# Transposing the FFN's hidden activations in 32x32 blocks on VectorE

## The chip, the cores and the metric

The kernel runs on one core of a Trainium2 chip. The metric is the device time of one execution in microseconds (us), taken as the median of several runs. The engines are TensorE (PE in the profile, PEld for its weight loads), VectorE (DVE), ScalarE (ACT), GpSimd (POOL) and SyncE (SP, which here only issues transfers).

## What is computed

One hybrid decoder layer on 256 tokens of width 2048, in float32: a half-step SwiGLU, a mixer (three attention groups side by side), and a second half-step SwiGLU. The change concerns the two SwiGLU blocks, which are these lines of the reference (D_MODEL = 2048, D_FF = 5632):

```
def swiglu(x, w_gate, w_up, w_down):
    return (jax.nn.silu(x @ w_gate) * (x @ w_up)) @ w_down
...
    x = x + 0.5 * swiglu(rms_norm(x, ffn1_norm[l]), ffn1_gate[l], ffn1_up[l], ffn1_down[l])
...
    x = x + 0.5 * swiglu(rms_norm(x, ffn2_norm[l]), ffn2_gate[l], ffn2_up[l], ffn2_down[l])
```

The hidden activations h = silu(gate) * up come out with tokens on the partitions, and the product with w_down needs them with the hidden index on the partitions. So h, 256 x 5632, is transposed once in each block.

## The kernel before, in words

**Precision by splitting.** Every weight and every activation that enters a large matmul is kept as two fp32r tiles: `hi`, a cast of the value, and `lo`, the value minus `hi`. A product is three matmuls: hi·hi, hi·lo, lo·hi (`mm_rows`, L272, L273, L274). A weight batch is 256 rows by 512 columns (`KB` = 2 tiles of 128 rows): one transfer from SP's queue into a tile `raw` (L218; four buffers), a cast on ACT into `hi` (L220; three buffers), a subtraction on DVE into `lo` (L221; three buffers), then 12 matmuls of 128x512, two token tiles by two row tiles by three. The second of the 12 is the first to read `lo`.

**Names.** `ag`, `au`, `ad` are gate, up and down weights of the first block, `bg`, `bu`, `bd` of the second, with the number of the batch's first row tile behind the name: `lo_ag_6` is the fourth batch of a gate chunk. `ga` and `ua` are the PSUM accumulators of gate and up.

**The loop.** `ffn` runs 11 chunks of 512 hidden columns. For each: gate, 8 weight batches; Silu on ACT into an SBUF tile `g` (L369, two halves of 128x512); up, 8 batches; and on DVE the product of up with `g` (L373, two halves), which leaves h for this chunk in `g`, with 128 tokens on the partitions. Then the down projection runs four chunks of 512 output columns, 22 batches each, reading `hT`, the transposed and split h.

**The transpose before.** `transpose_h` puts 8 TensorE transposes of 128x128 (L348) into one PSUM tile `th`, then calls `split` twice: ACT casts 128x512 out of PSUM into hT's hi half (L225), DVE subtracts into its lo half (L226).

**What sets the order.** `Lanes.tick()` is called after each weight batch and advances the queued side jobs by one `yield`. A job given to `lanes.put` waits for one of two lanes, each with a PSUM tile; one given to `lanes.run` needs no lane. The program's order is then a scheduler's: it may move instructions on an engine unless they are wrapped in `tc.keep_in_program_order`. Each engine runs its own list strictly in order. The lists are those shown in the section on the change.

Of the kernel before, what the change touches and what calls it, by code (L numbers as in the profile page):

```python
# [8 lines left out]
F32 = mybir.dt.float32  # L9
# [7 lines left out]
P = 128  # L17
D = 2048
NK = D // P
SEQ = 256  # L20
NT = SEQ // P
# [59 lines left out]
def hybrid_layer(ctx, tc, x, mem, ffn1_norm, ffn1_gate, ffn1_up, ffn1_down, mix_norm, mem_norm,  # L81
# [3 lines left out]
    nc = tc.nc  # L85

    x, mem, out = x[0], mem[0], out[0]
# [13 lines left out]
    def psum(tag, name):  # L101

        return ps.tile([P, 2, 512], F32, tag=tag, bufs=2 if tag == "acc" else 1, name=name)

    lanes = Lanes()
# [20 lines left out]
    ident = cpool.tile([P, P], F32, name="ident")  # L126
# [97 lines left out]
    def split(dst_hi, dst_lo, src):  # L224
        nc.scalar.copy(dst_hi, src)  # L225
        nc.vector.tensor_tensor(out=dst_lo, in0=src, in1=dst_hi.bitcast(F32), op=ALU.subtract)  # L226

    def transpose_chunk(xT, src, k0, nk, g0, name, pause=1, hi_dve=False, tag2=None):
# [24 lines left out]
            yield 1  # L253
        return stages

    def square_sums(ss, src, c):
        for t in range(NT):
            junk = small.tile([P, 512], F32, tag="junk", bufs=2, name="junk")
            tc.keep_in_program_order(
                nc.scalar.activation(junk, src[:, t, :], AF.Square, accum_out=ss[:, t, c:c + 1]))  # L260
# [15 lines left out]
    def project(acc, aT, w, c0, width, kts, nk_all, done, name, before=None):  # L276

        for k0, n in kts:
            k = k0
            while k < k0 + n:  # L280
                b = min(KB, k0 + n - k)
                if before:
                    before(k)
                wh, wl = load_w(w, k, b, c0, width, f"{name}_{k}")
                for j in range(b):
                    mm_rows(acc, aT, k + j, wh[:, j, :], wl[:, j, :], done == 0, done == nk_all - 1)
                    done += 1
                k += b
                lanes.tick()
        return done  # L290

    def project_end(acc, aT, w, c0, k0, n, name, landed):


        tiles = []
        for k in range(k0, k0 + n, KB):
            wh, wl = load_w(w, k, KB, c0, 512, f"{name}_{k}")
            tiles += [(wh[:, j, :], wl[:, j, :]) for j in range(KB)]
        for t in range(NT):
            for j, (wh, wl) in enumerate(tiles):  # L300
                hi, lo = (aT[:, k0 + j, i, t * P:(t + 1) * P] for i in range(2))
                nc.tensor.matmul(acc[:, t, :], hi, wh, start=False, stop=False)
                nc.tensor.matmul(acc[:, t, :], hi, wl, start=False, stop=False)
                nc.tensor.matmul(acc[:, t, :], lo, wh, start=False, stop=j == n - 1)
            for c, width in ((0, 256), (256, 256)) if t else ((0, 512),):
                landed(t, c, width)
        lanes.tick()

    def project_first(acc, aT, w, before, ready, name):


        batches = [(k, 1) for k in range(4)] + [(k, KB) for k in range(4, NK, KB)]

        def load(i):
            k, b = batches[i]
            before(k)
            return load_w(w, k, b, 0, 512, f"{name}_{k}", None if k else first_w)

        nxt = load(0)
        for i, (k, b) in enumerate(batches):  # L320
            (wh, wl), nxt = nxt, load(i + 1) if i + 1 < len(batches) else None
            ready(k)
            if k == 0:
                for a, v in ((0, wh), (1, wh), (0, wl)):
                    for t in range(NT):
                        nc.tensor.matmul(acc[:, t, :], aT[:, 0, a, t * P:(t + 1) * P], v[:, 0, :],
                                         start=a == 0 and v is wh, stop=False)
            else:
                for j in range(b):
                    mm_rows(acc, aT, k + j, wh[:, j, :], wl[:, j, :], False, k + j == NK - 1)  # L330
            lanes.tick()


    def ffn(xT, before, ready, stats, wg, wu, wd, after, last, name):


        with tc.tile_pool(name=f"h_{name}", bufs=1, reuse_waits="tile") as hpool, \
                tc.tile_pool(name=f"ht_{name}", bufs=2, reuse_waits="tile") as htmp:
            hT = hpool.tile([P, NF, 2, SEQ], F32R, name=f"hT_{name}")

            def transpose_h(j, h):

                def stages(tag):
                    tp = psum(tag, f"th_{name}{j}")
                    tv = tp.rearrange("p a b -> p (a b)").rearrange("p (k s) -> p k s", k=4)
                    for k in range(4):
                        for t in range(NT):
                            nc.tensor.transpose(tv[:, k, t * P:(t + 1) * P], h[:, t, k * P:(k + 1) * P],  # L348
                                                ident)
                    yield 1  # L350
                    for b in range(2):
                        f = slice(4 * j + 2 * b, 4 * j + 2 * b + 2)
                        split(hT[:, f, 0, :], hT[:, f, 1, :], tv[:, 2 * b:2 * b + 2, :])
                    yield 1
                return stages

            rstd = None
            for j in range(DFF // 512):
                acc = psum("acc", f"g{name}{j}")
                if j == 0 and ready:  # L360
                    project_first(acc, xT, wg, before, ready, f"{name}g{j}")
                else:
                    project(acc, xT, wg, j * 512, 512, [(0, NK)], NK, 0, f"{name}g{j}",
                            None if j else before)
                if j == 0:
                    rstd = stats()
                g = htmp.tile([P, NT, 512], F32, tag="g", bufs=3, name=f"gs{name}{j}")
                for t in range(NT):
                    nc.scalar.activation(g[:, t, :], acc[:, t, :], AF.Silu, scale=rstd[:, t:t + 1])  # L369
                acc = psum("acc", f"u{name}{j}")  # L370
                project(acc, xT, wu, j * 512, 512, [(0, NK)], NK, 0, f"{name}u{j}")
                for t in range(NT):
                    nc.vector.scalar_tensor_tensor(out=g[:, t, :], in0=acc[:, t, :],  # L373
                                                   scalar=rstd[:, t:t + 1], in1=g[:, t, :],
                                                   op0=ALU.mult, op1=ALU.mult)
                lanes.put(f"hT{name}{j}", transpose_h(j, g))

            def before_d(k):
                if k >= NF - 4:
                    lanes.finish(f"hT{name}{DFF // 512 - 1}")  # L380

            for c in range(4):
                acc = psum("acc", f"d{name}{c}")

                def landed(t, c0, width):
                    xc = x_sb[:, t, c * 512 + c0:c * 512 + c0 + width]
                    nc.vector.scalar_tensor_tensor(out=xc, in0=acc[:, t, c0:c0 + width], scalar=0.5, in1=xc,
                                                   op0=ALU.mult, op1=ALU.add)
                    after(c, t, c0, width)

                ending = 2 if last and c == 3 else 0
                project(acc, hT, wd, c * 512, 512, [(0, NF - ending)], NF, 0, f"{name}d{c}",
                        None if c else before_d)
                if ending:
                    project_end(acc, hT, wd, c * 512, NF - ending, ending, f"{name}d{c}", landed)
                else:
                    for t in range(NT):
                        landed(t, 0, 512)
# [34 lines left out]
    def sum_stages(ss, src, c, wait=None):  # L433
        yield 2 + c if wait is None else wait
        square_sums(ss, src(c), c)
# [17 lines left out]
    def mem_stages_T(c):  # L453
        def stages(tag):
            raw = mem_raw(c)
            yield 3
            yield from transpose_chunk(lambda: memTs[0], lambda: raw, 4 * c, 4, G_MEM, f"mem{c}")(tag)
            square_sums(ssm, raw, c)
        return stages
# [11 lines left out]
    def stats0():  # L471
        lanes.finish(*(f"ss0_{c}" for c in range(4)))
        return row_rstd(ss0, "x0")

    ffn(x0T, before0, ready0, stats0, gate1, up1, down1, after1, False, "a")
    memT = memTs[0]
    lanes.finish("memT3")


    with tc.tile_pool(name="mix", bufs=1, reuse_waits="tile") as mx, \  # L480
# [51 lines left out]
        sv = slots[:, 30:32, :]  # L532
# [216 lines left out]
        for half, (a, b) in (("a", (0, 3)), ("b", (3, 6))):  # L749
            for g, (c0, dst) in enumerate(((FOX_Q, fqT), (FOX_K, fkT))):  # L750
                name = f"f{'qk'[g]}{half}"
# [45 lines left out]
    def stats2():  # L797
        lanes.finish("ss2_3")
        return row_rstd(ss2, "x2")

    ffn(x2T, lambda k: lanes.finish("bT3") if k == 12 else None, None, stats2, gate2, up2, down2, store, True, "b")


# [29 lines left out]
```

## Time and profile before

| | us |
|---|---|
| median of 3 runs | 1833.43 (1833.03 to 1834.21) |
| the profiled execution, as timed | 1832.96 |
| its span, first to last instruction | 1831.3 |
| TensorE busy | 1821.4 (99%) |
| VectorE busy | 941.2 (51%) |
| ScalarE busy | 845.6 (46%) |

The profiled execution's own time lies 1.7 us above its span and 0.5 us below the median of the runs. Matmuls are pipelined, so the busy time of a matmul group counts overlaps of its own only; the distance from start to start is what one costs. An engine's idle time in front of an instruction is shown with what ended it.

### The profile page before, as it was taken

What the parts mean: (1) busy time and instruction counts of PE and PEld (TensorE: products, weight loads), DVE (VectorE), ACT (ScalarE), POOL (GpSimd) and SP (SyncE); (2) the same over time, 40 slices, a digit from 0 to 9 for tenths busy, and PEclk for the clock granted to TensorE, in tenths of its full rate; (3) what the DMA queues carried; (4) which work ended last, traced back from release to release, by engine and by line L of the source; (5) the groups of instructions that cost most, each with busy time, mean ns of one, the idle gap of its engine ahead of it and who ended that gap; (6) DMA issues with size and microseconds to landing.
All of it is one profiled execution on the core that took longest, in us unless ns stands there. A gap on an engine that the chain in (4) does not pass through costs nothing.

```text
span 1831.3 us, 21918 instructions
## 1 busy us (share of the span) xinstructions
PE 1821.4 (99%) x8434; PEld 1534.4 (84%) x8434; DVE 941.2 (51%) x1131; ACT 845.6 (46%) x1149; POOL 11.0 (1%) x31
## 2 busy tenths in 40 slices
PE   8999999999999999999999999999999999999998
PEld 7888888888888888888999888888888888888887
DVE  5545454545545454645666455455544444544443
ACT  6444444444435444557666454444444444433332
POOL 2000000000000000000000000000000000000000
PEclk9999999999999999999999999999999999999999
DMA  7666666666666566565656556666666666656664
GB/s 232 192 188 192 187 193 187 192 187 193 188 192 207 186 217 193 165 179 157 182 156 184 170 185 193 186 192 188 193 185 188 191 188 192 190 193 204 206 206 128
DMA packets 183144, 344.55 MB, mean 188 GB/s; under 512 B 11194, under 2 KB 28928, under 8 KB 182912
## 3 DMA queue, kind: packets, MB, share of 16 engines
q1 hardware_dynamic: 181488, 340.49, 62.1%
q0 software_dynamic: 528, 1.22, 0.3%
q10 hardware_dynamic: 1024, 1.45, 0.3%
q8 instruction: 66, 1.08, 0.3%
q14 instruction: 38, 0.31, 0.0%
HBM read 341.01 MB, written 2.11 MB: 187 GB/s over the span
## 4 chain that ended last, share of the span: by engine, by line
PE 98%; DMA 1%; ACT 1%; DVE 1%; issue 0%; ACTq 0%; DVEq 0%
PE ua L273 4%; PE da L274 4%; PE da L272 4%; PE gb L272 4%; PE gb L274 4%; PE gb L273 4%; PE ub L272 4%; PE ub L273 4%; PE ua L274 4%; PE ub L274 4%; PE da L273 4%; PE ua L272 4%; PE db L273 4%; PE db L274 4%; PE db L272 4%; PE ga L272 4%
## 5 line engine op out<-in xcount | busy, mean ns | idle before, releaser
L221 DVE TENSOR_TENSOR lo_bu<-raw_bu,hi_bu 128x1024 fp32r<-128x1024 f32 x88 | 107.8, 1225 | 131.5 <-ACT hi_bu L220 131.5
L221 DVE TENSOR_TENSOR lo_au<-raw_au,hi_au 128x1024 fp32r<-128x1024 f32 x88 | 107.8, 1225 | 126.2 <-ACT hi_au L220 126.2
L221 DVE TENSOR_TENSOR lo_bd<-raw_bd,hi_bd 128x1024 fp32r<-128x1024 f32 x88 | 107.8, 1225 | 124.0 <-ACT hi_bd L220 124.0
L221 DVE TENSOR_TENSOR lo_ad<-raw_ad,hi_ad 128x1024 fp32r<-128x1024 f32 x88 | 107.8, 1225 | 118.3 <-ACT hi_ad L220 118.3
L220 ACT CAST hi_bd<-raw_bd 128x1024 fp32r<-128x1024 f32 x88 | 92.8, 1055 | 145.0 <-PE db L274 139.8
L221 DVE TENSOR_TENSOR lo_bg<-raw_bg,hi_bg 128x1024 fp32r<-128x1024 f32 x88 | 107.7, 1224 | 99.4 <-ACT hi_bg L220 99.4
L221 DVE TENSOR_TENSOR lo_ag<-raw_ag,hi_ag 128x1024 fp32r<-128x1024 f32 (+1 forms) x89 | 107.3, 1206 | 97.7 <-ACT hi_ag L220 97.7
L220 ACT CAST hi_ad<-raw_ad 128x1024 fp32r<-128x1024 f32 x88 | 92.7, 1053 | 131.2 <-PE da L274 106.2
L220 ACT CAST hi_bg<-raw_bg 128x1024 fp32r<-128x1024 f32 x88 | 92.7, 1054 | 128.8 <-PE gb L274 70.0
L220 ACT CAST hi_ag<-raw_ag 128x1024 fp32r<-128x1024 f32 (+1 forms) x89 | 92.5, 1039 | 122.9 <-PE ga L274 66.3
L220 ACT CAST hi_bu<-raw_bu 128x1024 fp32r<-128x1024 f32 x88 | 92.8, 1054 | 115.5 <-PE ub L274 78.9
L220 ACT CAST hi_au<-raw_au 128x1024 fp32r<-128x1024 f32 x88 | 92.5, 1054 | 113.0 <-PE ua L274 79.1
L272 PE MATMUL gb<-hi_bg,x2T 128*128 128x512 f32 x352 | 137.9, 392 | 0.0
L272 PE MATMUL ga<-hi_ag,x0T 128*128 128x512 f32 x350 | 137.5, 393 | 0.0
L272 PE MATMUL da<-hi_ad,hT_a 128*128 128x512 f32 x352 | 137.4, 390 | 0.0
L273 PE MATMUL ua<-lo_au,x0T 128*128 128x512 f32 x352 | 137.1, 389 | 0.3 <-DVE lo_au L221 0.3
L274 PE MATMUL gb<-hi_bg,x2T 128*128 128x512 f32 x352 | 137.1, 389 | 0.0
L274 PE MATMUL da<-hi_ad,hT_a 128*128 128x512 f32 x352 | 137.0, 389 | 0.0
L273 PE MATMUL gb<-lo_bg,x2T 128*128 128x512 f32 x352 | 137.0, 389 | 0.0
L273 PE MATMUL da<-lo_ad,hT_a 128*128 128x512 f32 x352 | 136.9, 389 | 0.0
L272 PE MATMUL ua<-hi_au,x0T 128*128 128x512 f32 x352 | 136.9, 389 | 0.0
L274 PE MATMUL ua<-hi_au,x0T 128*128 128x512 f32 x352 | 136.9, 389 | 0.0
(478 smaller groups left out, 3957.7 us busy)
## 6 DMA issues: line engine op xcount, KB each, us to landing
raw_au<-in_ffn_up_dram SPq DMA_DIRECT2D x88, 512.0 KB, 3.7
raw_ad<-in_ffn_down_dram SPq DMA_DIRECT2D x88, 512.0 KB, 4.5
raw_bg<-in_ffn_gate_dram SPq DMA_DIRECT2D x88, 512.0 KB, 4.4
raw_bu<-in_ffn_up_dram SPq DMA_DIRECT2D x88, 512.0 KB, 3.7
raw_bd<-in_ffn_down_dram SPq DMA_DIRECT2D x88, 512.0 KB, 4.6
raw_ag<-in_ffn_gate_dram SPq DMA_DIRECT2D x86, 512.0 KB, 4.5
raw_wo<-in_w_out_dram SPq DMA_DIRECT2D x16, 512.0 KB, 3.7
raw_mk<-in_w_mem_k_dram SPq DMA_DIRECT2D x8, 512.0 KB, 3.7
```

The source lines that it names most:

```text
L220: nc.scalar.copy(h, r)
L221: nc.vector.tensor_tensor(out=l, in0=r, in1=h.bitcast(F32), op=ALU.subtract)
L272: nc.tensor.matmul(acc[:, t, :w], hi, wh, start=first, stop=False)
L273: nc.tensor.matmul(acc[:, t, :w], hi, wl, start=False, stop=False)
L274: nc.tensor.matmul(acc[:, t, :w], lo, wh, start=False, stop=last)
```

## The change

The 8 TensorE transposes of a chunk become 16 VectorE block transposes. One of them takes 32 partitions by 256 elements (2 token tiles x 4 column tiles x 32 columns): it transposes eight 32x32 blocks and writes them to another group of 32 partitions of a new SBUF tile `hr` (128x1024, one buffer). They come two to a `yield`, so two per weight batch as the program is written, and are pinned in program order on VectorE. The split reads `hr` in SBUF and not PSUM, as two stages after the eighth. The job goes through `lanes.run`, so it takes no lane and no PSUM tile. `g` has two buffers and not three; `hr` takes the same SBUF as the third.

```
+    def quad_transposes(dst, src):
+        sv = src.rearrange("p t (k b s) -> p b t k s", b=4, s=32)
+        dv = dst.rearrange("p k (t a s) -> p a t k s", t=NT, s=32)
+        for a in range(4):
+            for b in range(4):
+                tc.keep_in_program_order(
+                    nc.vector.transpose(out=dv[32 * b:32 * b + 32, a], in_=sv[32 * a:32 * a + 32, b]))
+                if b % 2:
+                    yield 1
...
-                def stages(tag):
-                    tp = psum(tag, f"th_{name}{j}")
-                    tv = tp.rearrange("p a b -> p (a b)").rearrange("p (k s) -> p k s", k=4)
-                    for k in range(4):
-                        for t in range(NT):
-                            nc.tensor.transpose(tv[:, k, t * P:(t + 1) * P], h[:, t, k * P:(k + 1) * P],
-                                                ident)
+                raw = htmp.tile([P, 4, SEQ], F32, tag="raw", bufs=1, name=f"hr_{name}{j}")
+                yield from quad_transposes(raw, h)
+                for b in range(2):
+                    f = slice(4 * j + 2 * b, 4 * j + 2 * b + 2)
+                    split(hT[:, f, 0, :], hT[:, f, 1, :], raw[:, 2 * b:2 * b + 2, :])
                     yield 1
-                    for b in range(2):
-                        f = slice(4 * j + 2 * b, 4 * j + 2 * b + 2)
-                        split(hT[:, f, 0, :], hT[:, f, 1, :], tv[:, 2 * b:2 * b + 2, :])
-                    yield 1
-                return stages
...
-                g = htmp.tile([P, NT, 512], F32, tag="g", bufs=3, name=f"gs{name}{j}")
+                g = htmp.tile([P, NT, 512], F32, tag="g", bufs=2, name=f"gs{name}{j}")
...
-                lanes.put(f"hT{name}{j}", transpose_h(j, g))
+                lanes.run(f"hT{name}{j}", transpose_h(j, g))
```

On **VectorE**, around the end of the first chunk's up projection and the first batches of the second chunk's gate, the list before is this:

```order
L221 TENSOR_TENSOR lo_ag_2_617<-raw_ag_2_615,hi_ag_2_616 128x1024
L373 SCALAR_TENSOR_TENSOR gsa_430<-ua_433,y_x_416,gsa_430 128x512 x2
L221 TENSOR_TENSOR lo_ag_4_639<-raw_ag_4_637,hi_ag_4_638 128x1024
L221 TENSOR_TENSOR lo_ag_6_657<-raw_ag_6_655,hi_ag_6_656 128x1024
L226 TENSOR_TENSOR hT_a<-th_a_606,hT_a 128x2x256 x2
L221 TENSOR_TENSOR lo_ag_8_675<-raw_ag_8_673,hi_ag_8_674 128x1024
```

and now this (`hr_a` is the new tile, `gsa` is `g`):

```order
L221 TENSOR_TENSOR lo_ag_2_611<-raw_ag_2_609,hi_ag_2_610 128x1024
L377 SCALAR_TENSOR_TENSOR gsa_430<-ua_433,y_x_416,gsa_430 128x512 x2
L221 TENSOR_TENSOR lo_ag_4_631<-raw_ag_4_629,hi_ag_4_630 128x1024
L263 STREAM_TRANSPOSE hr_a_606<-gsa_430 32x2x4x32 x6
L221 TENSOR_TENSOR lo_ag_6_651<-raw_ag_6_649,hi_ag_6_650 128x1024
L263 STREAM_TRANSPOSE hr_a_606<-gsa_430 32x2x4x32 x2
L221 TENSOR_TENSOR lo_ag_8_671<-raw_ag_8_669,hi_ag_8_670 128x1024
```

It goes on in the same way, two block transposes ahead of each `lo`, to the first batch of up:

```order
L221 TENSOR_TENSOR lo_ag_14_731<-raw_ag_14_729,hi_ag_14_730 128x1024
L263 STREAM_TRANSPOSE hr_a_606<-gsa_430 32x2x4x32 x2
L221 TENSOR_TENSOR lo_au_0_755<-raw_au_0_753,hi_au_0_754 128x1024
L226 TENSOR_TENSOR hT_a<-hr_a_606,hT_a 128x2x256 x2
L221 TENSOR_TENSOR lo_au_2_775<-raw_au_2_773,hi_au_2_774 128x1024
```

Six block transposes stand in a row ahead of `lo_ag_6`, then two ahead of each of the next five `lo`, and the split has moved from behind `lo_ag_6` to behind `lo_au_0`, five batches later. Every chunk of both blocks has this pattern; behind the eleventh the names are those of the down weights.

On **ScalarE**, at the same place, the list before is this:

```order
L220 CAST hi_ag_4_638<-raw_ag_4_637 128x1024
L220 CAST hi_ag_6_656<-raw_ag_6_655 128x1024
L225 CAST hT_a<-th_a_606 128x2x256 x2
L220 CAST hi_ag_8_674<-raw_ag_8_673 128x1024
L220 CAST hi_ag_10_692<-raw_ag_10_691 128x1024
```

and now, five batches on, this:

```order
L220 CAST hi_ag_14_730<-raw_ag_14_729 128x1024
L220 CAST hi_au_0_754<-raw_au_0_753 128x1024
L225 CAST hT_a<-hr_a_606 128x2x256 x2
L220 CAST hi_au_2_774<-raw_au_2_773 128x1024
L373 ACTIVATE gsa_749<-ga_587,y_x_416 128x512 x2
```

The two casts of the split have moved to the boundary of gate and up, just ahead of `hi_au_2` and the Silu.

On **TensorE** the 22 groups of 8 transposes are gone and nothing else has moved. SP's and GpSimd's lists are the same as before.

## Rows read from the trace of the kernel before

**Rows 1.** The page: span, busy time, the slices of TensorE and its clock

```profile
span 1831.3 us, 21918 instructions
PE 1821.4 (99%) x8434; PEld 1534.4 (84%) x8434; DVE 941.2 (51%) x1131; ACT 845.6 (46%) x1149; POOL 11.0 (1%) x31
...
PE   8999999999999999999999999999999999999998
...
PEclk9999999999999999999999999999999999999999
```

**Rows 2.** The chain that ended last: shares by engine, one piece (start, length)

```profile
PE 98%; DMA 1%; ACT 1%; DVE 1%; issue 0%; ACTq 0%; DVEq 0%
...
60.52 0.87 PE th_a L348 x8
```

**Rows 3.** Line 348 (TensorE's transposes): ns min/median/max, first and last start

```profile
L348 PE MATMUL th_a<-ident,gsa x88: 270/272/273, 60.4 to 505.3; 128*128 128x128 f32 x88
...
L348 PE MATMUL th_b<-ident,gsb x88: 270/272/273, 1144.4 to 1589.3; 128*128 128x128 f32 x88
```

**Rows 4.** Timeline of TensorE from one transpose group to the next: start, length

```profile
60.36 1.03 PE L348 MATMUL th_a<-ident,gsa 128*128 128x128 f32 x8
61.15 0.48 PE L272 MATMUL ga<-hi_ag,x0T 128*128 128x512 f32 x1
61.47 0.40 PE L273 MATMUL ga<-lo_ag,x0T 128*128 128x512 f32 x1
...
104.32 0.39 PE L273 MATMUL ga<-lo_ag,x0T 128*128 128x512 f32 x1
104.78 1.03 PE L348 MATMUL th_a<-ident,gsa 128*128 128x128 f32 x8
```

**Rows 5.** That stretch: length, busy time by engine (instructions), clock, DMA share, GB/s

```profile
60.36:104.78 44.42, 44.42 (x202) 36.87 (x200) 22.22 (x21) 19.08 (x20) 0.00 (x0) 1.00 0.64 189
```

**Rows 6.** Timeline of VectorE there: start, length, in brackets idle time before

```profile
57.84 1.41 DVE L373 SCALAR_TENSOR_TENSOR gsa<-ua,y_x,gsa 128x512 f32<-128x512 f32 x2 [0.41 <-PE ua L274]
59.17 1.22 DVE L221 TENSOR_TENSOR lo_ag<-raw_ag,hi_ag 128x1024 fp32r<-128x1024 f32 x1
61.64 1.23 DVE L221 TENSOR_TENSOR lo_ag<-raw_ag,hi_ag 128x1024 fp32r<-128x1024 f32 x1 [1.26 <-ACT hi_ag L220]
```

**Rows 7.** Timeline of ScalarE there

```profile
57.84 1.06 ACT L220 CAST hi_ag<-raw_ag 128x1024 fp32r<-128x1024 f32 x1 [1.67 <-PE ua L274]
60.56 1.05 ACT L220 CAST hi_ag<-raw_ag 128x1024 fp32r<-128x1024 f32 x1 [1.67 <-PE ga L274]
61.51 0.58 ACT L225 CAST hT_a<-th_a 128x512 fp32r<-128x512 f32 x1
```

**Rows 8.** VectorE's groups by form: count, busy us, mean ns, idle before

```profile
L561 DVE TENSOR_SCALAR ss_m<-ss_m,ri_m 128x256 f32<-128x256 f32 x8 | 2.4, 350 | 0.1
...
L613 DVE SCALAR_TENSOR_TENSOR ss_f<-s_f,cq,nck_all 128x256 f32<-128x256 f32 x6 | 2.8, 475 | 0.0
...
L221 DVE TENSOR_TENSOR lo_ag<-raw_ag,hi_ag 128x512 fp32r<-128x512 f32 x3 | 2.1, 686 | 0.0
...
L221 DVE TENSOR_TENSOR lo_au<-raw_au,hi_au 128x1024 fp32r<-128x1024 f32 x88 | 107.8, 1225 | 126.2 <-ACT hi_au L220 126.2
...
L226 DVE TENSOR_TENSOR hT_a<-th_a,hT_a 128x512 fp32r<-128x512 f32 x22 | 15.1, 687 | 7.2 <-ACT hT_a L225 7.2
```

**Rows 9.** The tile raw_ag: ns min/median/max of its readers, us to landing

```profile
L220 ACT CAST hi_ag<-raw_ag x89: 607/1055/1060, 5.8 to 472.1; 128x1024 fp32r<-128x1024 f32 x86, 128x512 fp32r<-128x512 f32 x3
...
DMA to landing us min/median/max: 3.7/4.5/9.1
```

**Rows 10.** SP's queue, its waits: total us, times, longest

```profile
SPq L218 <- DVE lo_ag L221: 197.4, 83, 3.2
```

## The prediction

> **What bounds the kernel now.** I read the page first, then the chain of waits, then the timelines around one transpose group. [...] In the stretch from one group to the next TensorE has no idle time at all (44.42 of 44.42 us), while VectorE works 22.22 and ScalarE 19.08 [rows 5]. So there is work on TensorE that nothing covers, and half of VectorE's time is free. What must be seen in the timelines is how long VectorE may be occupied with something else before a `lo` comes too late; that decides whether the free half can be used.
>
> **What is removed.** Line 348 has 88 transposes in each block, 22 groups of 8 in all [rows 3]. What a group costs is not the 1.03 us of its row, since neighbours overlap, nor eight times 272 ns, but the distance it adds. From group to group it is 104.78 - 60.36 = 44.42 us, and in between lie the 192 matmuls of a gate and an up chunk. Their own pace is read away from the group: the second of them starts at 61.47, the last but one at 104.32 [rows 4]; that is 189 steps in 42.85 us, 0.2267 us each. 192 steps are 43.53 us, and the group adds 44.42 - 43.53 = 0.89 us. The chain's 0.87 agrees [rows 2]. The last group of each block lies in the down projection, at the end of the stretch of line 348 [rows 3], where the weight stream is of the same make; I count it the same. Sum: 22 x 0.89 = 19.6 us off TensorE. All of it is on the path.
>
> **What is added on VectorE.** 16 block transposes a chunk, 352 in all, of 256 elements on 32 partitions. Call the cost of one, start to start, T. The trace has no block transpose. Nearest rows at 256 elements: a scaling from SBUF to SBUF takes 350 ns, a two-input operation that reads PSUM takes 475 [rows 8]. The two subtractions of 512 and 1024 elements, 686 and 1225 ns, give 1.05 ns an element and 0.15 us fixed [rows 8]; by that, 256 elements cost 0.42 at one step an element, 0.69 at two (the 686 row), 1.22 at four (the 1225 row). I take 0.45 us, since the rows of that size lie on both sides of it, and keep 0.35 and 1.22 as ends. At 0.45 the chunk's 16 are 7.2 us, and VectorE's load rises from 22.2 to 29.4 of 43.5 us: room enough on average.
>
> [...]
>
> **When a `lo` is late.** The lists put six block transposes ahead of `lo_ag_6`, and two ahead of each of the next five. Before, `lo_ag_4` ends at 59.17 + 1.22 = 60.39, and `lo_ag_6` waits for its cast until 61.64 [rows 6], which itself waits for TensorE to give a `hi` buffer back [rows 7]. Now VectorE starts the six at 60.39, and `lo_ag_6` ends at 60.39 + 6T + 1.23. TensorE needs it for the second matmul of that batch: the gate's first batch ends at 60.36 [rows 4], two batches of 12 x 0.2267 = 2.72 us follow, then one step, 66.03. So 6T may be 4.41: T up to 0.735. At T = 0.45 `lo_ag_6` ends at 64.32, 1.7 us early. After that each batch adds 2T + 1.23 against 2.72, which gains 0.6 us a batch at 0.45. By `lo_au_0`, 16 transposes and six subtractions after 60.39, the bound is 60.39 + 16T + 7.35 <= 66.03 + 13.60, T up to 0.743. So up to about 0.74 the transposes cost nothing; the cover is the two batches by which `lo` runs ahead of TensorE. Past it a chunk loses 16T - 11.9 us.
>
> **The other parts.** The split moves behind `lo_au_0` on VectorE and behind `hi_au_0` on ScalarE. Its subtractions read SBUF and not PSUM: 687 ns before, 686 ns for the same size from SBUF [rows 8]. Its casts are 0.58 us each from PSUM [rows 7]; the least of the casts from SBUF, the one of that size, is 0.607 [rows 9]; so two are 1.2 us, and ScalarE idles 1.67 us ahead of each `hi` in the steady stream [rows 7]. They wait for the sixteenth block transpose, and `hi_au_2` and the Silu stand behind them. That transpose ends some 2.2 us after `hi_ag_14` does (1.23 for `lo_ag_14`, 0.9 for two), and `hi_au_0` ends 2.72 after it, so they find it done. If not, the cover is again the two batches' lead. The first block transpose waits for `g` on its own engine, just made; the one buffer of `hr` was read by the split a gate's length earlier; the second `g` back has been transposed long before. All these cost nothing. SP's transfers of `raw` wait for the `lo` four batches earlier, a mean of 2.4 us a time now (197.4 / 83) [rows 10]. `lo_ag_6` comes 1.4 us later than before (64.32 for 62.87), a transfer lands 4.5 us after its issue [rows 9], at 68.8, and its cast cannot start before TensorE is through with the batch three before it, at 71.2. The margin is 2.4 us. Finally, h no longer takes a lane or a PSUM tile; nothing else on TensorE moved, so no gain or loss from it.
>
> **The sum.** The profiled execution took 1832.96 us; less 19.6 it is 1813.4. The median of the runs is 0.47 above that execution, so I forecast 1833.43 - 19.6 = 1813.8 us.
>
> **The rivals.**
> 1. *VectorE too slow, the kernel slower.* The mechanism is the six in a row and then two a batch on an in-order engine; the place is `lo_ag_6` to `lo_au_0` of each chunk (and the down batches behind the eleventh). It starts at T = 0.74 and cancels the gain where 16T - 11.9 = 0.89, T = 0.80. At 1.22 a chunk loses 7.6 - 0.89 = 6.7 us net, and the kernel takes 1833.4 + 22 x 6.7 = 1981 us. Against it: no row of VectorE at this size is above 0.48, and at two steps an element T is still 0.69. For it: no row shows the operation, a quarter of the lanes may have a fixed cost of its own, and the margin at 0.69 is only 0.3 us. [...] Chance 0.11.
> 2. *Just above the bound*, T from 0.74 to 0.80: part of the gain is lost, 1814 to 1833 us, in the middle 1823. Chance 0.05.
> 3. *The weight stream takes the gain.* If transfers or casts were what sets the pace, 2% less time per chunk would turn into waits of TensorE. The transfers would have to go from 189 GB/s to 193 [rows 5], with DMA at 0.64 of its time; ScalarE's `hi` wait for TensorE's buffers and not for landings [rows 7]. Then 1825 to 1834 us, with no change at the far end. Chance 0.05.
> 4. *The change doesn't take the transposes off the path*: the lists show that they are gone and that nothing took their place on TensorE. I give it nothing of its own.
>
> **How the numbers follow.** The forecast has 0.79: any T from 0.35 to 0.74 gives the same time, so its own range is that of the median's spread (0.8 us) and of the group's cost (0.87 to 0.89, 0.4 us in all): 1812 to 1816. To be at 8 in 10 the range takes in part of rival 2: 1812 to 1822. About 0.2%, or 3.7 us, is what a measurement of this kernel can tell from no change. Faster by more: 0.79 and most of rivals 2 and 3, 0.84; within: 0.04; slower: 0.12, rival 1 and a little for what I have not seen.
>
> **What would show it.** In the profile after: TensorE with about 176 fewer matmuls and still no idle time in the gate and up chunks, 43.5 us from chunk to chunk; the block transposes at 0.42 to 0.5 us, VectorE at some 1100 us busy (941 + 352 x 0.45); `lo_ag_6` ending well ahead of its matmul, and transfers still waiting for `lo`. I am wrong if the block transpose takes more than 0.74 us: then TensorE waits for `lo` ahead of the second matmul of a batch, from the fourth gate batch on; or if TensorE waits for `lo` because its cast was held by the split's casts or a landing: then ScalarE's idle time ahead of `hi` is ended by VectorE or by a transfer and not by TensorE.

## The result, and the profile after

The changed kernel takes **1814.01 us** (median of 4 runs, 1813.86 to 1815.92) against 1833.23 for the kernel before beside it: a ratio of 0.9898, with a 95% interval of 0.9885 to 0.9910. That is 19.2 us less, where 19.6 were forecast (1813.8 us). The profiled execution took 1814.06 us, 1.8 above its span.

The page after, to be laid beside [rows 1] and the first line of [rows 2]: span, busy time, the slices of TensorE, VectorE and the clock, the shares of the chain.

```profile
span 1812.3 us, 21918 instructions
PE 1802.0 (99%) x8258; PEld 1517.1 (84%) x8258; DVE 1091.0 (60%) x1483; ACT 845.0 (47%) x1149; POOL 10.8 (1%) x31
...
PE   8999999999999999999999999999999999999998
...
DVE  5666666666655454645665455666666666654443
...
PEclk9999999999999999999999999999999999999999
...
PE 98%; DMA 1%; ACT 1%; DVE 1%; issue 0%; ACTq 0%; DVEq 0%
```

TensorE has 176 instructions fewer and is as full as before: the chain is still 98% TensorE. VectorE has 150 us more work (941 to 1091), and yet the kernel ends earlier.

One chunk of the first block, from its first gate matmul to the next chunk's; length, then busy time of TensorE, its weight loads, VectorE, ScalarE, GpSimd, then the clock, DMA's share and GB/s. It answers to [rows 5].

```profile
57.86:101.38 43.52, 43.52 (x193) 36.07 (x192) 29.02 (x36) 19.07 (x20) 0.00 (x0) 1.00 0.66 193
```

44.42 us a chunk has become 43.52, the 192 matmuls alone. VectorE went from 22.2 to 29.0 us.

What one block transpose takes (count, ns min/median/max, first and last start):

```profile
L263 DVE STREAM_TRANSPOSE hr_a<-gsa x176: 425/436/442, 60.5 to 509.7; 32x256 f32<-32x256 f32 x176
```

VectorE's timeline of the first such chunk, which answers to [rows 6]:

```profile
59.39 1.22 DVE L221 TENSOR_TENSOR lo_ag<-raw_ag,hi_ag 128x1024 fp32r<-128x1024 f32 x1
60.53 2.67 DVE L263 STREAM_TRANSPOSE hr_a<-gsa 32x256 f32<-32x256 f32 x6
63.23 1.23 DVE L221 TENSOR_TENSOR lo_ag<-raw_ag,hi_ag 128x1024 fp32r<-128x1024 f32 x1
64.49 0.89 DVE L263 STREAM_TRANSPOSE hr_a<-gsa 32x256 f32<-32x256 f32 x2
65.41 1.23 DVE L221 TENSOR_TENSOR lo_ag<-raw_ag,hi_ag 128x1024 fp32r<-128x1024 f32 x1
...
70.03 1.23 DVE L221 TENSOR_TENSOR lo_ag<-raw_ag,hi_ag 128x1024 fp32r<-128x1024 f32 x1 [0.31 <-ACT hi_ag L220]
```

and ScalarE's at the end of the same gate, which answers to [rows 7]:

```profile
74.38 1.05 ACT L220 CAST hi_au<-raw_au 128x1024 fp32r<-128x1024 f32 x1 [1.66 <-PE ga L285]
75.34 1.14 ACT L225 CAST hT_a<-hr_a 128x512 fp32r<-128x512 f32 x2
77.15 1.05 ACT L220 CAST hi_au<-raw_au 128x1024 fp32r<-128x1024 f32 x1 [0.67 <-ACT hT_a L225]
```

The six in a row take 2.67 us, 0.445 each from start to start. `lo_ag_6` ends at 64.46; its matmul is due at 66.25 here (the gate's first matmul at 57.86, three batches of 2.72 us, one step), so it is 1.8 us early. After that VectorE catches up, and by `lo_ag_12` (the row at 70.03) it waits for ScalarE's cast again. The casts of the split take their place in front of `hi_au_2` without a wait for the transposes, and fill 1.0 of the 1.7 us that ScalarE had idle there. TensorE waits for no `lo` in these stretches: in both kernels its longer waits are some single ones at the start (2.5 us), in the mixer (0.5 us) and at the end (0.8 us).

### The profile page after: what moved, and what is told of

The parts are those of the page before. It is cut to its first block, busy times and chain, and to the rows that moved or that the text cites. A ratio compares the mean times of both kernels' runs of the same rounds, so it can differ in the third digit from the quotient of the medians.

```text
span 1812.3 us, 21918 instructions
## 1 busy us (share of the span) xinstructions
PE 1802.0 (99%) x8258; PEld 1517.1 (84%) x8258; DVE 1091.0 (60%) x1483; ACT 845.0 (47%) x1149; POOL 10.8 (1%) x31
## 3 DMA queue, kind: packets, MB, share of 16 engines
q0 software_dynamic: 528, 1.22, 0.3%
q8 instruction: 64, 1.05, 0.2%
## 4 chain that ended last, share of the span: by engine, by line
PE 98%; DMA 1%; ACT 1%; DVE 1%; issue 0%; ACTq 0%; DVEq 0%
PE ua L284 4%; PE da L284 4%; PE da L283 4%; PE gb L284 4%; PE ub L283 4%; PE ub L284 4%; PE gb L283 4%; PE da L285 4%; PE ua L285 4%; PE gb L285 4%; PE ub L285 4%; PE ua L283 4%; PE db L285 4%; PE db L284 4%; PE db L283 4%; PE ga L283 4%
## 5 line engine op out<-in xcount | busy, mean ns | idle before, releaser
L284 PE MATMUL ub<-lo_bu,x2T 128*128 128x512 f32 x352 | 137.1, 390 | 0.0
L285 PE MATMUL ub<-hi_bu,x2T 128*128 128x512 f32 x352 | 137.1, 390 | 0.0
L283 PE MATMUL ub<-hi_bu,x2T 128*128 128x512 f32 x352 | 137.1, 390 | 0.0
```

The lines of the kernel that those rows point to most:

```text
L283: nc.tensor.matmul(acc[:, t, :w], hi, wh, start=first, stop=False)
L284: nc.tensor.matmul(acc[:, t, :w], hi, wl, start=False, stop=False)
L285: nc.tensor.matmul(acc[:, t, :w], lo, wh, start=False, stop=last)
```

## The experiments

All times are medians, beside runs of the kernel before of 1833.2 to 1833.4 us. The changed kernel is at 1814.0.

| run | what differs from the changed kernel | us | ratio to the kernel before, 95% |
|---|---|---|---|
| none | no transpose of h at all | 1813.58 | 0.9892 (0.9878 to 0.9907) |
| both | TensorE's transposes back, as dead work | 1833.70 | 1.0002 (0.9992 to 1.0011) |
| rep24 | 24 block transposes a chunk | 1814.02 | 0.9894 (0.9879 to 0.9909) |
| rep26 | 26 a chunk | 1821.10 | 0.9933 (0.9918 to 0.9948) |
| rep32 | 32 a chunk | 1863.17 | 1.0163 (1.0146 to 1.0180) |
| row16 | 16, all in a row | 1910.79 | 1.0420 (1.0404 to 1.0435) |
| half | 32 of half the size | 1813.86 | 0.9895 (0.9880 to 0.9910) |
| unpinned | no pin in program order | 1813.89 | 0.9893 (0.9879 to 0.9908) |
| x12 | four more groups on VectorE | 1815.23 | 0.9901 (0.9884 to 0.9917) |
| three | three more groups | 1813.28 | 0.9890 (0.9874 to 0.9907) |

**Is it TensorE's time alone?** Two runs ask from both sides: one leaves the transposes out altogether, one has both kinds.

```
-                yield from quad_transposes(raw, h)
+                for _ in range(8):
+                    yield 1
...
-                    split(hT[:, f, 0, :], hT[:, f, 1, :], raw[:, 2 * b:2 * b + 2, :])
+                    split(hT[:, f, 0, :], hT[:, f, 1, :],
+                          h[:, b, :].rearrange("p (k s) -> p k s", k=2))
```

> No transpose of h at all, on either engine: the split reads g as it lies, so the down projection multiplies untransposed blocks (the transpose is left out of the computation, the rest is done). If the 352 block transposes are wholly hidden behind TensorE, this takes the same time as the changed kernel, 1814.0 us, within 1 us. If they cost something that no wait shows (a slower matmul pace, a late start), it is faster by that: a rival that blames them for the 0.6 us by which the measured gain in the span (19.0 us) falls short of the 19.6 forecast gives 1813.4 or less.

```
                 lanes.run(f"hT{name}{j}", transpose_h(j, g))
+                lanes.put(f"pe{name}{j}", pe_transposes(j, g))
```

(`pe_transposes` is the old transpose into PSUM, without the split. `none` leaves the transpose out of the computation; the rest is done.)

> The changed kernel with the 22 groups of 8 TensorE transposes put back as dead work (they write a PSUM tile that nobody reads) while h still goes through VectorE. If the gain is TensorE time alone, this gives it back whole: 1814.0 + 22 x 0.87 to 0.89 = 1833.2 to 1833.6 us. If part of the gain came from elsewhere in the change (the split read from SBUF, its later place, the lane and the PSUM tile that h no longer takes), it stays below 1833 by that part.

The run without transposes takes 1813.58 us, 0.4 less than the changed kernel; the one with both takes 1833.70, which gives back 19.7 (0.1 above the expected range). The chunk's length shows the same, here for `none` and then for `both`:

```profile
57.91:101.43 43.52, 43.52 (x194) 36.04 (x192) 22.12 (x20) 19.06 (x20) 0.00 (x0) 1.00 0.67 194
```

```profile
57.67:102.08 44.41, 44.41 (x201) 36.88 (x200) 29.02 (x36) 19.05 (x20) 0.00 (x0) 1.00 0.65 191
```

With VectorE's transposes or without, 43.52 us; with TensorE's, 44.41, though VectorE does 29.02 us of work in it as well. So VectorE's transposes are hidden in the chunks, and the gain is TensorE's time; neither the later split nor its source in SBUF adds to it. The 0.4 us between `none` and the changed kernel don't lie in the chunks. In the two profiles (0.5 us apart) they are two single late `lo`, 0.3 us in the first block's down projection and 0.3 in the mixer. This is the first one on TensorE in the changed kernel, where 0.227 us is the pace:

```profile
638.12 0.39 PE L283 MATMUL da<-hi_ad,hT_a 128*128 128x512 f32 x1
638.50 0.50 PE L284 MATMUL da<-lo_ad,hT_a 128*128 128x512 f32 x1
638.84 0.39 PE L285 MATMUL da<-hi_ad,hT_a 128*128 128x512 f32 x1
```

Each follows a transfer that landed later than in `none`, with ScalarE or VectorE waiting for it, and VectorE then works without a pause up to the late `lo`:

```profile
632.45 1.05 ACT L220 CAST hi_ad<-raw_ad 128x1024 fp32r<-128x1024 f32 x1 [0.17 <-DMA raw_ad<-in_ffn_down_dram]
884.29 0.56 DVE L571 TENSOR_TENSOR nck_all<-nck_all,cmask 128x384 f32<-128x384 f32 x1 [0.89 <-DMA nck_all<-nck_dram]
```

No block transpose stands near either, and the profile of `unpinned`, which has all 352, shows neither of the two. What made the transfers late in this execution stays open.

**How many would fit?** The cover was said to be the two batches by which `lo` runs ahead of TensorE, and its end the deadline of each single `lo`. Repeating some of the block transposes into the same place adds work to VectorE and nothing else.

```
-                tc.keep_in_program_order(
-                    nc.vector.transpose(out=dv[32 * b:32 * b + 32, a], in_=sv[32 * a:32 * a + 32, b]))
+                for _ in range(2):       # rep32; rep26: 2 if b % 2 or a == 3 else 1; rep24: 2 if b % 2 else 1
+                    tc.keep_in_program_order(
+                        nc.vector.transpose(out=dv[32 * b:32 * b + 32, a], in_=sv[32 * a:32 * a + 32, b]))
```

> Ten of the 16 block transposes of a chunk are done twice: 26 a chunk, 8 ahead of lo_ag_6 and then 3, 3, 4, 4, 4. At 0.445 us from start to start that is 11.57 us. In the trace of the changed kernel the six start at 60.53, a lo takes 1.265 us with its gaps, and lo_au_0 is due at 66.25 + 13.60 = 79.85: room for 26.4 transposes. So the lead of two batches should just cover it: 1814 us, at most 1816. If each microsecond on VectorE cost TensorE something, 10 more transposes would show: even a tenth of their 4.45 us in each of 22 chunks is 10 us, 1824.

> 24 block transposes a chunk (eight done twice): 8 ahead of lo_ag_6, then 3, 3, 4, 3, 3. With 26, lo_au_0 came 0.18 us too late in each chunk (its matmul started at 80.00 and not at 79.82). Two fewer free 0.89 us, so every lo is in time by 0.7 us: 1814 us, within 1. If the 26 lost their 7 us to the load on VectorE and not to that one deadline, some 80% of it stays: 1819 to 1820.

> Every block transpose done twice: 32 a chunk, 14.2 us, which lie 11 ahead of lo_ag_6, then 2, 6, 2, 6, 2, 3. VectorE's load is then 36 of 43.5 us a chunk, so if only the average counted nothing would be lost: 1814 us. By the deadlines of the single lo, lo_ag_6 is late by 0.4 us, lo_ag_10 by 1.1 and lo_ag_14 (27 transposes ahead, room for 23.1) by 1.7 us; TensorE waits 1.7 us a chunk: 1814 + 22 x 1.7 = 1852 us, 1840 to 1865, which is slower than the kernel before.

24 cost nothing (1814.02), 26 cost 7.1 us, 32 cost 49.2. The expectation for 26 was missed, by less than a transpose: in its trace the last four transposes of a chunk end too late for `lo_au_0`. VectorE's rows, then TensorE's around the matmul that needs it:

```profile
73.73 1.83 DVE L264 STREAM_TRANSPOSE hr_a<-gsa 32x256 f32<-32x256 f32 x4
75.59 1.22 DVE L221 TENSOR_TENSOR lo_ag<-raw_ag,hi_ag 128x1024 fp32r<-128x1024 f32 x1
76.85 1.84 DVE L264 STREAM_TRANSPOSE hr_a<-gsa 32x256 f32<-32x256 f32 x4
78.72 1.23 DVE L221 TENSOR_TENSOR lo_au<-raw_au,hi_au 128x1024 fp32r<-128x1024 f32 x1
```

```profile
79.37 0.39 PE L286 MATMUL ga<-hi_ag,x0T 128*128 128x512 f32 x1
79.59 0.39 PE L284 MATMUL ua<-hi_au,x0T 128*128 128x512 f32 x1
80.00 0.50 PE L285 MATMUL ua<-lo_au,x0T 128*128 128x512 f32 x1
80.34 0.40 PE L286 MATMUL ua<-hi_au,x0T 128*128 128x512 f32 x1
```

`lo_au_0` ends at 79.95, and its matmul starts at 80.00 where the pace would have had it at 79.82. The next one follows 0.34 us later and not 0.23: 0.18 + 0.11 is 0.29 us a chunk, and 7.1 / 22 is 0.32. My count of 26.4 took 1.265 us for a `lo` with its gaps, which is right (75.59 to 76.85), but 0.445 us for a transpose: up to the start of what follows, a chunk's 26 take 11.94 us, 0.459 each (four take 1.86 in the rows above; 0.453 each in the changed kernel), which is 0.37 us more than counted. The 32 wait at three places of a chunk, and each wait costs the 0.11 us again, 7 us in all, which is most of why 1852 was too low:

```profile
66.78 0.50 PE L285 MATMUL ga<-lo_ag,x0T 128*128 128x512 f32 x1 [0.43 <-DVE lo_ag L221]
...
72.96 0.50 PE L285 MATMUL ga<-lo_ag,x0T 128*128 128x512 f32 x1 [0.45 <-DVE lo_ag L221]
...
79.15 0.50 PE L285 MATMUL ga<-lo_ag,x0T 128*128 128x512 f32 x1 [0.41 <-DVE lo_ag L221]
```

**Load or place?** The sharpest form: the same 16, in one stage.

```
         for a in range(4):
             for b in range(4):
                 tc.keep_in_program_order(...)
-                if b % 2:
-                    yield 1
+        for _ in range(8):
+            yield 1
```

> The same 16 block transposes per chunk, but all in one stage: the list has 16 in a row between lo_ag_4 and lo_ag_6, and none later. VectorE does the same work as in the changed kernel. If only its load counted, 1814 us. By the deadlines lo_ag_6 ends at 60.53 + 16 x 0.445 + 1.23 = 68.9 us where the second matmul of its batch is due at 66.25: TensorE waits 2.6 us in every chunk, and by the run with 32 a stall costs some 0.1 us more in the matmuls behind it, so 22 x 2.75 = 60 us: 1874, 1865 to 1885. A wait of TensorE for lo_ag (the fourth batch) and no other would show.

VectorE works no longer than in the changed kernel (1087 us), and the kernel takes 1910.79 us, 97 more. VectorE's 16, and TensorE's matmul that waits for `lo_ag_6` behind them:

```profile
60.45 7.17 DVE L263 STREAM_TRANSPOSE hr_a<-gsa 32x256 f32<-32x256 f32 x16
67.65 3.50 DVE L221 TENSOR_TENSOR lo_ag<-raw_ag,hi_ag 128x1024 fp32r<-128x1024 f32 x3
```

```profile
65.95 0.39 PE L283 MATMUL ga<-hi_ag,x0T 128*128 128x512 f32 x1
68.93 0.50 PE L284 MATMUL ga<-lo_ag,x0T 128*128 128x512 f32 x1 [2.59 <-DVE lo_ag L221]
```

The step is 2.98 us and not 0.23, so 2.75 + 0.11 us a chunk, 63 us in 22. The rest, 34 us between the medians, the expectation did not have. It is in the clock. The same run, behind the first chunk's wait and around the second's, columns as above (the clock stands behind GpSimd's busy time):

```profile
69.00:72.00 3.00, 3.00 (x13) 2.48 (x14) 3.00 (x4) 0.99 (x3) 0.00 (x0) 1.00 0.67 186
...
112.00:115.00 3.00, 0.74 (x4) 0.28 (x2) 2.92 (x6) 0.94 (x2) 0.00 (x0) 1.00 0.00 0
115.00:116.00 1.00, 0.66 (x2) 0.62 (x3) 1.00 (x2) 1.00 (x2) 0.00 (x0) 0.83 0.00 0
116.00:117.00 1.00, 1.00 (x4) 0.72 (x4) 1.00 (x2) 0.15 (x1) 0.00 (x0) 0.50 0.62 102
...
118.00:119.00 1.00, 1.00 (x4) 0.81 (x3) 0.76 (x2) 0.00 (x0) 0.00 (x0) 0.50 1.01 311
119.00:120.00 1.00, 1.00 (x5) 0.75 (x5) 0.00 (x0) 0.25 (x1) 0.00 (x0) 0.96 0.91 293
```

Behind the first wait the clock stays at full grant (1.00); behind the second, as long, it stands at half (0.50) for 3.4 us, from 0.3 us after TensorE has started again. Eight matmuls go at 0.43 us each in that time (115.68 to 116.10 is one such step) and not 0.23: 1.6 us. The 21 waits after the first one each have such a stretch of 3.4 us with them; it begins between 0.4 us before TensorE's restart and 1.3 us after it, and those chunks are 1.4 to 1.6 us longer than the first one's, 31 us in all. With the 63 us that is the 94 us by which the profiled execution (1908.57, the fastest of the four) lies above the changed kernel; the 2 us more of the median have no profile.

**What is a block transpose's price made of?**

```
-                tc.keep_in_program_order(
-                    nc.vector.transpose(out=dv[32 * b:32 * b + 32, a], in_=sv[32 * a:32 * a + 32, b]))
+                for t in range(NT):
+                    tc.keep_in_program_order(
+                        nc.vector.transpose(out=dv[32 * b:32 * b + 32, a, t], in_=sv[32 * a:32 * a + 32, b, t]))
```

> Each block transpose cut into two of 128 elements (one token tile each), 32 a chunk, four to a stage; the list has 8 ahead of lo_ag_4 and 4 ahead of each of the next six lo. This measures the price of one. If it is 0.15 us fixed and 1.05 ns an element, as the two-input rows of VectorE have it, one of 128 is 0.285 to 0.30 us start to start, a chunk's 32 are 9.6 us, every lo is still in time, and the kernel stays at 1814 us, within 1. If the price is mostly fixed (0.44 at 128 too), the 32 are 14 us and the time is that of the run with 32, 1863 us or more.

1813.86 us, no change. The row of the half-size ones (ns min/median/max), and then eight of them in the timeline:

```profile
L264 DVE STREAM_TRANSPOSE hr_a<-gsa x352: 255/278/308, 60.5 to 511.2; 32x128 f32<-32x128 f32 x176
```

```profile
60.45 2.01 DVE L264 STREAM_TRANSPOSE hr_a<-gsa 32x128 f32<-32x128 f32 x8
```

They come at 0.25 us each on the mean, less than the 0.285 to 0.30 expected. The price per element of one is as it was taken: 0.30 us for the first of two small ones (the longer; the second, which overlaps it, takes 0.26) and 0.436 for the large make 1.06 ns an element and 0.16 us fixed, where the subtractions gave 1.05 and 0.15 [rows 8]: one step an element by that measure. The small ones overlap in pairs: two with the same group of source partitions and of destination partitions take 0.48 to 0.50 us together, while the large ones, each with another destination group than the one in front, start only when that one has ended (the six above, 0.436 us long, come every 0.445). Whether the partitions are the reason, or the order of the pairs, was not tried by itself.

**Does the pin matter?**

```
-                tc.keep_in_program_order(
-                    nc.vector.transpose(out=dv[32 * b:32 * b + 32, a], in_=sv[32 * a:32 * a + 32, b]))
+                nc.vector.transpose(out=dv[32 * b:32 * b + 32, a], in_=sv[32 * a:32 * a + 32, b])
```

> The block transposes without the pin in program order. The scheduler then puts 6 ahead of lo_ag_6, and 3, 5 and 2 ahead of the next three, the split two batches earlier. Cumulated that is 6, 9, 14, 16 where the deadlines leave room for about 9.9, 13.2, 16.5, 19.8: no lo is late, so 1814 us, within 1. If the pin is what makes the change work, this is slower.

1813.89 us: it doesn't, since the order without it (6, 3, 5, 2) is in time as well.

**Can more be moved?** The chunks of x that are transposed for the mixer and for the second block cost TensorE 0.87 us a group too (two that stand on the chain before, at 1055.24 and 1077.45, have this length).

```
+    def quad_chunk(pool, xT, src, k0, g0, name, pace=2):
+        raw = pool.tile([P, 4, SEQ], F32, tag="q", name=f"qr_{name}")
+        yield from quad_transposes(raw, src, pace)
+        for k in range(4):
+            ...
-            lanes.put(f"bT{c}", transpose_chunk(...))
+            if c < 3:        # x12; in the run called three: c < 2
+                lanes.run(f"bT{c}", quad_chunk(mt, x2T, xchunk(c), 4 * c, G_FFN2, f"x2_{c}", 4 if c == 2 else 2))
+            else:
+                lanes.put(f"bT{c}", transpose_chunk(...))
```

(and the same for the first chunk of x1T.)

> The same device used for four more groups: the first 512 columns of the mixer's input and the first three quarters of the second FFN's input are transposed on VectorE too, in 16 block transposes each, into a tile that the heads use elsewhere, and scaled and split from there. Four groups of 8 TensorE transposes go: 4 x 0.87 = 3.5 us, so 1810.5 us if VectorE's lists leave room there. VectorE also has the heads' and the attention's work at those places; if a lo comes late there, or the next stage waits for its transposed input, the gain is smaller or gone: 1812 to 1818.

> As the run with four more groups, but the third quarter of the second FFN's input goes back to TensorE: its 12 block transposes in a row ahead of one lo made TensorE wait 2.5 us there, and the clock fell after it. Three groups remain on VectorE, and their lists have at most 8 in a row ahead of a lo. If the deadlines are all that matters, three groups of TensorE transposes are saved: 3 x 0.87 = 2.6 us, so 1811.4 us, 1810.5 to 1812.5. If VectorE's work in the attention stages is the limit, 1814 or more.

Four groups made it slower than the changed kernel (1815.23). The third of the second block's four has four transposes to a stage, and the list put 12 in a row ahead of one `lo`. VectorE's row, and TensorE's:

```profile
1067.89 5.37 DVE L263 STREAM_TRANSPOSE qr_x<-x_sb 32x256 f32<-32x256 f32 x12
```

```profile
1074.57 0.79 PE L297 MATMUL wo<-lo_wo,mixT 128*128 128x512 f32 x1 [2.51 <-DVE lo_wo L221]
1075.16 0.63 PE L298 MATMUL wo<-hi_wo,mixT 128*128 128x512 f32 x1
1075.58 0.63 PE L296 MATMUL wo<-hi_wo,mixT 128*128 128x512 f32 x1
```

A wait of 2.5 us, and here the clock falls with a single one:

```profile
1075.00:1076.00 1.00, 1.00 (x3) 0.72 (x3) 0.97 (x3) 0.00 (x0) 0.00 (x0) 0.50 0.18 41
```

With that group back on TensorE the run takes 1813.28 us (1812.99 to 1813.48), where 1811.4 was expected. That is 0.7 less than the changed kernel and the lowest median of all, though hardly more than the 0.5 us that the two late `lo` above cost one execution; 1.9 of the 2.6 us are gone again. Two of the jobs overlap in the output projection, their transposes lie four to a batch with their scaling behind, and `lo` comes 0.1 to 0.2 us late in five batches running:

```profile
1054.77 0.39 PE L296 MATMUL wo<-hi_wo,mixT 128*128 128x512 f32 x1
1055.19 0.50 PE L297 MATMUL wo<-lo_wo,mixT 128*128 128x512 f32 x1
1055.53 0.39 PE L298 MATMUL wo<-hi_wo,mixT 128*128 128x512 f32 x1
```

(0.42 and 0.34 us where 0.23 each is the pace.) The five come to 1.3 us, and one remaining transpose group waits another 0.5 us for its chunk of x.

## Why the prediction was right

**What bounds the kernel** held: TensorE's work alone sets the time, and its transposes lay on it whole. `both` gives the 19.7 us back.

**The term removed** was 0.89 us a group, 19.6 in all. The chunk is 0.90 shorter (44.42 to 43.52), 19.8 us in 22. The medians show 19.2 and the two spans 19.0: the profiled execution after is 0.2 us later by the second chunk's first gate matmul (57.86 for 57.64), before any group, and the two late `lo` cost it 0.5. The nearness of 19.6 is in part luck, since two small errors are of opposite sign: a group was set down 0.01 us too small, and nothing was set down for a later start or a late `lo`.

**The price of a block transpose**, the one operation that no row showed, was taken as 0.45 from rows at the same size; it is 0.445 to 0.46 from start to start. That this met so well is not what made the forecast right: by the prediction's own bound any price up to 0.735 gives the same time, so one step an element or two would have done, and four would not. The end of 1.22 (four steps an element) was far off. The lower end, 0.35, came from a scaling, which is faster at the same size than any block transpose was (0.425 at the least).

**The cover** was named rightly, and its size nearly: T up to 0.743 in the sum, 11.9 us for a chunk's transposes. In `rep26` they take 11.94 us and `lo_au_0` is 0.18 us late for its matmul, so there was room for 11.76, T up to 0.735. The term that is short is the 7.35 us for six subtractions: with the gaps between them they take 7.5.

**The other parts at no cost** held too. The casts take 0.618 us each from SBUF (0.607 taken, 0.581 from PSUM before) and found the sixteenth transpose done; SP's transfers still wait for `lo` (188.1 us in 83 waits, 197.4 before [rows 10]).

**The rival that did not come**, a VectorE too slow, has its mechanism confirmed by `rep32` (1863.17 us, waits of 0.41 to 0.45) and `row16` (1910.79 us, waits of 2.6): in-order transposes ahead of a `lo`. Its price was too low, since it had neither the 0.11 us behind a wait nor the clock. The weight stream took nothing: it went from 189 to 193 GB/s.

**The faster engine** for the transpose is TensorE by these runs (0.90 us a chunk against 7.1 on VectorE), and still the wrong one, because its time is the only time that counts here.

## What to carry to other kernels

In this kernel, work moved from a full engine to one that is half idle was free as long as no single instruction behind it came late. So count what lies in front of each due instruction on the receiving engine, not the load. The same 16 transposes gained 19 us when spread and lost 78 against the kernel before when put in a row. Here an operation that no trace showed could be priced from rows of the same element count on the same engine, and a repeat of it inside the kernel showed afterwards how much room is left.

## What the runs showed of the hardware

- A float32 block transpose on VectorE took 0.436 us for 256 elements on each of 32 of the 128 partitions (the changed kernel) and 0.30 for 128 (`half`), which is 0.16 us and 1.06 ns an element by these two sizes: a chunk's 16 took 7.1 us, where the subtraction of as many elements took 1.2.
- A matmul that had to wait for its operand was followed by the next one 0.11 us later than in the stream (0.34 for 0.23 us) while the clock was full, after the shortest waits seen here (0.2 us, `rep26`) as after the longest (2.6 us, the first chunk of `row16`).
- Waits of TensorE of 2.5 to 2.6 us came with a stretch of half clock, of 3.4 us each, in `x12` (one wait) and in `row16` from the second chunk on, while the 0.4 us waits of `rep32` left the granted clock at 0.999 on the mean. The first wait of `row16` had no such fall with it; why is open.
